# Sixty-four bytes: which columns of the low weight parts are displaced in the two feed-forward products of a hybrid decoder layer

## The chip, the cores and the metric

The kernel runs on one core of one Trainium2 chip. The metric is device time in microseconds (us) of one execution; lower is better. TensorE multiplies, VectorE (DVE) and ScalarE (ACT) prepare operands and take results away, SyncE (SP) and GpSimd (POOL) issue transfers.

## What is computed

One decoder layer on 512 tokens of width 2048: adaLN modulation, a combined projection, a short convolution beside an attention with three branches, an output projection, and then the feed-forward part, in which the change lies:

```python
h = modulate(rms_norm(x, norm2_g[l]), sh2, sc2)
x = x + g2[:, None, :] * (jnp.square(jax.nn.relu(h @ w_ff1[l])) @ w_ff2[l])
return rms_norm(x, normf_g)
```

`w_ff1` is 2048 by 8192 and `w_ff2` 8192 by 2048, all in fp32.

## The kernel before

**Split numbers.** An fp32 operand is split into a high part (rounded to the type fp32r) and a low part (the rest). A product of two operands takes three matmuls, high by high, high by low and low by high (`mm3`, line 347). ScalarE writes the high part (`nc.scalar.activation(..., AF.Copy)`), VectorE the low part as the difference of the raw weight and the high part (`hilo`, line 1097).

**Seven products instead of eight.** Each feed-forward product is cut into blocks of two by two and done with seven block products (Winograd's form of Strassen's scheme): `operands` (line 1230) makes from four raw weight blocks seven operands, in the order B1, U6, T5, B2, T7, B3, T4, with four additions on VectorE (tiles `sg`, `rw`) and seven splits (tiles `hl`). Four raw blocks with their seven operands are called a pair here. The code counts pairs as `p` in the first product (`ff1`, line 1277; pairs 3 to 31, pairs 0 to 2 being done in another form by `part`, line 1347, with weights from `make`, line 1326) and as `4 * f + q` in the second (line 1443; pairs 0 to 30, the last block by `plain`, line 1421).

An operand is 128 rows by 8 blocks of 128 columns, k = 0 to 7. For each column block `run` (line 1246) issues three matmuls of 256 tokens, so an operand is 24 matmuls, a pair 168. The token tiles are `tk`, the accumulators `pf` (eight PSUM banks). In the second product the eight column blocks go to two results, four each.

**Where the weights lie.** The weight operands live in a ring of three tiles `hl` of 2048 + 64 fp32 numbers per partition (line 1046). The high part lies at the front, the low part 4096 bytes behind it. `SHIFT` is 16 numbers, 64 bytes. Three layouts exist, picked by `stage_of`: in the output projection (0) nothing is shifted; in the first feed-forward product (1) high and low are both shifted by 64 bytes, and in the third tile of the ring, the last column block of the low part lies 64 bytes further (`[1] * 7 + [2]`); in the second product (2) the third tile has its last four column blocks of the low part 64 bytes further (`[1] * 4 + [2] * 4`). So in the first product every third operand has one displaced column block, in the second every third has four. Class `Low` (line 1048) turns a column into its place. Where one column block is displaced, VectorE writes the low part in two instructions, of 896 and of 128 columns; where four are, one instruction with a two-part pattern does it (2 x 512). The split weights of the second half of the output projection (`kept`, line 1139) also use layout 1 for three tiles.

**What sets the order.** All instructions of this part are recorded by the class `Order` (line 47) and then emitted in the order that its planner finds: TensorE's order is the program's, the other engines take what is ready and most urgent, by cost formulas (`price`, line 91) and due times. Each engine then works strictly in its emitted order. An `hl` tile can be refilled only after TensorE has read it, three operands back; raw weights have six buffers (`rw`). In the second product VectorE also adds each result to the residual, six updates and one sum for each of two results in a pair (`update`, line 1384); in the last four blocks (`f == 7`) it adds the pieces of the final norm as well (`final`, `shared`). During the first pairs of the second product, SyncE also reads back the residual (`residual_pairs`, line 1409), and the last pieces of the first product (`outcome`, line 1260) are still being written.

Of the kernel before, what the change touches and what calls it, by code (L numbers as in the profile page):

```python
# [31 lines left out]
SHIFT = 16  # L32
# [241 lines left out]
def hybrid_layer(ctx: ExitStack, tc: tile.TileContext, a, out):  # L274
    nc = tc.nc
# [17 lines left out]
    nc = order = Order(tc, xs[0].tensor.tag, NMAIN, passes=6)  # L293
# [21 lines left out]
    class lane:  # L315

        def __init__(self, n):
            self.n = n
# [59 lines left out]
    ring = [slot(name="wa")[:, :1024] for _ in range(NWA)]  # L378
# [201 lines left out]
    w = weights(a["w_kv"][0])  # L580
# [8 lines left out]
    for s, (name, k) in enumerate(steps[:-1]):  # L589
# [6 lines left out]
        for n in range(8):  # L596
            c = slice(n * P, (n + 1) * P)
# [3 lines left out]
        if s + 1 < len(steps):  # L601

            nxt = steps[s + 1][1]
            if s >= 4:
                w = blob(s + 1)
# [3 lines left out]
            if s < 4:  # L609
                w = blob(s + 1)  # L610
# [152 lines left out]
    for j in range(8):  # L763
        if j % 2 == 0:
            ys.append(pair(name="y"))
        y = ys[-1][:, j % 2]
        got = []
        for i in range(3):
            n = 3 * j + i
# [30 lines left out]
    for g in range(NG):  # L800
        pv = [bank() for _ in range(NQ)]
        for blk in range(4):
            wh, wl = weights(a["w_v"][g * 4 + blk], BLOB)
            more_ada(1)
            for j in range(4):
                k = blk * 4 + j
                s = slice(j * 268, (j + 1) * 268)
                for t in range(NQ):
                    c = slice(t * P, (t + 1) * P)
# [5 lines left out]
        for t in range(NQ):  # L815
            if t % 2 == 0:
# [4 lines left out]
                                    in1=vv[g, t][:, 0].bitcast(F32), op=OP.subtract)  # L821
# [66 lines left out]
    nc = tc.nc  # L888
    temps = cycle(ts)
    nc = order = Order(tc, mix[0].tensor.tag, NMAIN, passes=6)  # L890
# [149 lines left out]
    nc = order = Order(tc, x1[0].tensor.tag, NMAIN)  # L1040
    ffn = ExitStack()
    ffp = ffn.enter_context(tc.tile_pool(name="ffp", bufs=2, reuse_waits="tile"))
    psf = ffn.enter_context(tc.tile_pool(name="psf", bufs=8, space=PSUM, reuse_waits="tile"))
    HT = T // 2
    rw = cycle([ffp.tile([P, 1024], F32, name="rw", bufs=6) for _ in range(6)])
    hl = [ffp.tile([P, 2048 + 4 * SHIFT], F32R, name="hl", bufs=3) for _ in range(3)]

    class Low:

        def __init__(self, t, places):  # L1050
            self.t, self.places = t, places

        def __getitem__(self, at):
            a, b = at[1].start, at[1].stop
            o = 1024 + self.places[a // P] * SHIFT
            return self.t[:, o + a:o + b]

        def parts(self):
            cut = [k for k in range(1, 8) if self.places[k] != self.places[k - 1]]
            if cut == [4]:  # L1060
                n = 512 + (self.places[4] - self.places[0]) * SHIFT
                o = 1024 + self.places[0] * SHIFT
                yield slice(0, 1024), self.t[:, o:o + 2 * n].rearrange("p (a b) -> p a b", a=2)[:, :, :512], 2
                return
            for a, b in zip([0] + cut, cut + [8]):
                c = slice(a * P, b * P)
                yield c, self[:, c], 1

    def ring(high, *low):
        return cycle([[t[:, high * SHIFT:high * SHIFT + 1024], Low(t, p)] for t, p in zip(hl, low)])  # L1070

    rings = [ring(0, [0] * 8, [0] * 8, [0] * 8), ring(1, [1] * 8, [1] * 8, [1] * 7 + [2]),
             ring(1, [1] * 8, [1] * 8, [1] * 4 + [2] * 4)]
    stage_of = [0]
    ffp.tile([P, SHIFT], F32, name="shift", bufs=1)
    sg = {t: cycle([ffp.tile([P, 1024], d, name="sg", bufs=2) for _ in range(2)])
          for t, d in (("first", F32R), ("sums", F32), ("last", F32R))}
# [13 lines left out]
        nc.sync.dma_start(out=raw, in_=src)  # L1091
        return raw

    def hl_tile():
        return [next(q) for q in rings][stage_of[0]]

    def hilo(dst, src, minus=False):
        nc.scalar.activation(dst[0], src, AF.Copy, scale=-1.0 if minus else 1.0)
        for c, low, n in dst[1].parts() if isinstance(dst[1], Low) else [(slice(0, 1024), dst[1], 1)]:
            x, h = src[:, c], dst[0][:, c].bitcast(F32)  # L1100
            if n > 1:
                x, h = (y.rearrange("p (a b) -> p a b", a=n) for y in (x, h))
            if minus:
                nc.vector.scalar_tensor_tensor(out=low, in0=x, scalar=-1.0, in1=h, op0=OP.mult, op1=OP.subtract)
            else:
                nc.vector.tensor_tensor(out=low, in0=x, in1=h, op=OP.subtract)
        return dst

    def square_into(sacc, xm, c, first):
# [25 lines left out]
        if i % 2:  # L1135
            nc.gpsimd.dma_start(out=x1d[i // 2], in_=x1[i // 2])

    stage_of[0] = 1
    kept = []
    for i in range(8):  # L1140
        if i < 3:
            dst = hl_tile()
        elif i == 3:
            dst = [next(sg["first"]) for _ in range(2)]
        elif i == 4:
            dst = [next(gt).rearrange("p a b c -> p (a b c)")
                   for _ in range(2)]
# [79 lines left out]
                tok[i][q] = tslot()  # L1227
                tsplit(tok[i][q], t)

    def operands(raw, minus=False):  # L1230

        a11, a21, a22, a12 = raw
        s1, s2 = [next(sg["sums"]) for _ in range(2)]
        sub(s1, a21, a22, OP.add)
        sub(s2, s1, a11, OP.add)
        yield hilo(hl_tile(), a11)
        yield hilo(hl_tile(), s2)
        yield hilo(hl_tile(), s1, minus)
        yield hilo(hl_tile(), a12)
        sub(a21, a21, a11, OP.add)  # L1240
        yield hilo(hl_tile(), a21)
        sub(s2, s2, a12, OP.add)
        yield hilo(hl_tile(), s2)
        yield hilo(hl_tile(), a22)

    def run(ps, w, toks, first, last, base=0, n=8, c=LO):
        wh, wl = w
# [29 lines left out]
    def ff1(p):  # L1277
        raw = [raw_blob(a["w_f1"][p, b]) for b in range(4)]
        ps = {}
        x, y = temp((P, 2, HT), name="gx"), temp((P, 2, HT), name="gy")  # L1280
        for i, w in enumerate(operands(raw, True)):
# [24 lines left out]
        outcome(p, x, y, [temp((P, 2, HT), name="gz") for _ in range(2)])  # L1306
# [19 lines left out]
    def make(n):  # L1326
        p, b = plan[n][:2]
        if n == 1:
            dst = [next(sg["first"]) for _ in range(2)]
        elif n == 3:  # L1330
            dst = [next(gt).rearrange("p a b c -> p (a b c)")
                   for _ in range(2)]
        else:
            dst = hl_tile()
        made[n] = hilo(dst, raw_blob(a["w_f1"][p, b]))

    def results_of(p):
# [101 lines left out]
                    final(m, halves[hf])  # L1439
            finish(hf)  # L1440

    stage_of[0] = 2
    for f in range(8):
        for i in range(7):
            for j in range(2):
# [5 lines left out]
        for q in range(3 if last else 4):  # L1451
            raw = [raw_blob(a["w_f2"][4 * f + q, b]) for b in range(4)]
            ps = [{}, {}]
            for i, w in enumerate(operands(raw)):
# [125 lines left out]
```

## Time and profile before

| what | value |
|---|---|
| time before, median of 3 runs | 2130.83 us (2130.73 to 2131.65) |
| the profiled execution's own time | 2131.37 us |
| its span, first to last instruction | 2129.6 us |
| mean granted TensorE clock | 0.991 |
| busy: TensorE, VectorE, ScalarE | 97%, 89%, 47% of the span |
| matmuls of 128 x 256 tokens on `hl` weights, `pf<-tk,hl` | 10704 |

How to read it: the profile of one execution gives for each instruction when it started and how long it took. The start is measured; the end of a matmul is modelled. Matmuls are pipelined, so one that lasts 276 ns does not keep the next waiting that long, and a busy TensorE says nothing about its pace: the pace is how many matmuls start in a stretch. A table by stretches of time gives each engine's busy time and, behind an x, the number of its instructions that touch the stretch. In it the first feed-forward product's full pairs run from about 930 to 1483 us, the second product from 1483 to about 2115 us.

### The profile page before, as it was taken

To read this page: it belongs to the slowest core of one execution; us is meant where nothing else is said; L and a number is where in the kernel's file an instruction comes from. 1 tells how busy PE (TensorE), PEld (TensorE's weight loads), DVE (VectorE), ACT (ScalarE), POOL (GpSimd) and SP (SyncE) were. 2 spreads that over 40 slices of the span, in tenths; PEclk is the share of its full clock that TensorE was granted. 3 is DMA by queue.
4 is the path that set the end of the run, shared out by engine and by line. 5 is a ranking of instruction groups with operands and counts; after the bars stand their busy time and mean duration, and the time that the engine had idled before them with its cause. 6 is when DMAs were issued, how large, how long until landed. Compare 5 with 4: busy or idle time off the path is not lost.

```text
span 2129.6 us, 38017 instructions
## 1 busy us (share of the span) xinstructions
PE 2071.7 (97%) x15014; PEld 1930.5 (91%) x15014; DVE 1889.5 (89%) x3045; ACT 1008.6 (47%) x1470; POOL 128.6 (6%) x244
## 2 busy tenths in 40 slices
PE   5999999999999999999999999999999999999997
PEld 3888778898877779999999999999999999999997
DVE  8989888887987656999999999999999999999998
ACT  4532333222454434766666666666433333333345
POOL 0000000000000001021221211111000000000000
PEclk8999999999999999999999999999999999999999
DMA  8995679888321144477766677669876366366452
GB/s 333 346 352 221 217 279 326 308 292 314 108 80 40 50 139 158 129 228 208 221 201 202 199 218 215 202 206 306 309 268 230 128 247 236 130 239 237 136 182 90
DMA packets 144130, 454.17 MB, mean 213 GB/s; under 512 B 15824, under 2 KB 20176, under 8 KB 143952
## 3 DMA queue, kind: packets, MB, share of 16 engines
q1 hardware_dynamic: 108816, 386.72, 52.5%
q0 software_dynamic: 34048, 63.98, 9.5%
q8 instruction: 118, 1.93, 0.4%
q10 hardware_dynamic: 1088, 1.05, 0.1%
q14 instruction: 60, 0.49, 0.1%
HBM read 383.53 MB, written 68.16 MB: 212 GB/s over the span
## 4 chain that ended last, share of the span: by engine, by line
PE 55%; DVE 1%; ACT 1%; issue 0%; DMA 0%; DVEq 0%; ACTq 0%
PE pf L120 55%; DVE x L120 0%; DVE hl L120 0%; ACT t L120 0%; ACT x L120 0%; DMA rw<-in_w_f 0%; DVE rw L120 0%; DVE sg L120 0%; DVE sacc L120 0%; ACT hl L120 0%; DVE t L120 0%; ACT tk L120 0%; DVE gt L120 0%; DVEq L1576 0%; ACT sacc L120 0%
## 5 line engine op out<-in xcount | busy, mean ns | idle before, releaser
L120 PE MATMUL pf<-tk,hl 128*128 128x256 f32 x10704 | 1235.5, 278 | 2.3 <-ACT t L120 1.4
L120 PEld LDWEIGHTS pf<-tk,hl 128*128 128x128 f32 x10704 | 1233.6, 188 | 3.1 <-ACT t L120 1.6
L120 ACT ACTIVATE hl<-rw 128x1024 fp32r<-128x1024 f32 x269 | 285.4, 1062 | 337.5 <-PE pf L120 302.7
L120 DVE TENSOR_TENSOR hl<-rw,hl 128x1024 fp32r<-128x1024 f32 (+2 forms) x314 | 331.9, 1064 | 36.5 <-ACT hl L120 36.5
L120 ACT ACTIVATE hl<-sg 128x1024 fp32r<-128x1024 f32 x180 | 191.1, 1062 | 230.1 <-PE pf L120 203.5
L120 PE MATMUL ps<-h_m,wh 128*128 128x512 f32 x1080 | 252.6, 390 | 0.0
L120 DVE SCALAR_TENSOR_TENSOR t<-wa,cs 128x1024 bf16<-128x1024 f32 x192 | 234.2, 1220 | 20.0 <-DMA wa<-in_w_ada 18.0
L120 PEld LDWEIGHTS ps<-h_m,wh 128*128 128x128 f32 x1080 | 201.6, 188 | 41.5
L120 ACT ACTIVATE wh<-raw 128x1024 fp32r<-128x1024 f32 (+1 forms) x106 | 112.7, 1063 | 251.8 <-PE ps L120 204.1
L120 DVE TENSOR_TENSOR hl<-sg,hl 128x1024 fp32r<-128x1024 f32 (+2 forms) x170 | 185.6, 1101 | 31.8 <-ACT hl L120 31.1
L120 PE MATMUL ps<-h,wh 128*128 128x512 f32 x840 | 200.7, 395 | 5.7 <-ACT h L120 3.3
L120 PEld LDWEIGHTS ps<-h,wh 128*128 128x128 f32 x840 | 159.1, 191 | 41.6 <-ACT h L120 5.3
L120 DVE TENSOR_TENSOR wh<-raw,wh 128x1024 fp32r<-128x1024 f32 (+1 forms) x106 | 129.9, 1226 | 24.3 <-ACT wh L120 23.5
L120 DVE SCALAR_TENSOR_TENSOR x<-pf,mod,x 128x256 f32<-128x256 f32 (+1 forms) x280 | 133.6, 486 | 17.7 <-PE pf L120 16.7
L120 DVE TENSOR_TENSOR sg<-sg,rw 128x1024 f32<-128x1024 f32 x120 | 146.0, 1217 | 0.1
L120 POOL DMA_DIRECT2D g<-gt x192 | 101.5, 533 | 408.6 <-ACT hl L120 237.7
L120 PE MATMUL pw<-mix,wh 128*128 128x512 f32 x384 | 109.8, 406 | 0.0
L120 ACT ACTIVATE t<-t 128x512 f32<-128x512 f32 (+3 forms) x131 | 74.7, 571 | 16.3 <-DVE t L120 14.3
L120 PEld LDWEIGHTS pw<-mix,wh 128*128 128x128 f32 x384 | 69.7, 190 | 11.0 <-issue 0.5
L120 DVE TENSOR_TENSOR sg<-rw 128x1024 f32<-128x1024 f32 x60 | 73.0, 1217 | 7.2 <-DMA rw<-in_w_f 4.8
L120 DVE TENSOR_TENSOR rw<-rw 128x1024 f32<-128x1024 f32 x60 | 72.9, 1216 | 0.0
L120 DVE TENSOR_TENSOR gt<-t,gt 128x512 fp32r<-128x512 f32 x96 | 65.5, 683 | 2.0 <-PE pf L120 1.1
(204 smaller groups left out, 1782.4 us busy)
## 6 DMA issues: line engine op xcount, KB each, us to landing
rw<-in_w_f SPq DMA_DIRECT2D x263, 512.0 KB, 3.9
wa<-in_w_ada SPq DMA_DIRECT2D x192, 512.0 KB, 6.0
tk<-g SPq DMA_DIRECT2D x114, 512.0 KB, 5.9
g<-gt POOLq DMA_DIRECT2D x192, 256.0 KB, 4.6
raw<-in_w_conv SPq DMA_DIRECT2D x32, 512.0 KB, 5.0
x<-in_xt SPq DMA_DIRECT2D x16, 512.0 KB, 5.3
raw<-in_w_kv SPq DMA_DIRECT2D x16, 512.0 KB, 4.6
raw<-in_w_cv SPq DMA_DIRECT2D x16, 512.0 KB, 3.8
```

Of the source, the lines that this page charges most:

```text
L120: x.i, x.eng, x.call = len(self.nodes), eng, (lambda: real(*args, **kw))
```

## The change

The three layouts go. There is one ring of three tiles, with a place (0 before the first feed-forward product, 1 from there on) that shifts high and low parts alike, and a flag per operand, `moved`: with it the last column block of the low part, and only that, lies 64 bytes further. It is set

- for the operands that `make` prepares (blocks 0 to 2 of the first product),
- for all seven operands of pairs with a number below 6: pairs 3, 4 and 5 of the first product, 0 to 5 of the second,
- for one operand in each later pair, operand i where i is the pair's number modulo 7,
- for no other: not for `kept`, and not in `plain`.

VectorE writes a moved low part in two instructions (896 and 128 columns), any other in one; the form 2 x 512 is gone. The core of the diff:

```diff
-    hl = [ffp.tile([P, 2048 + 4 * SHIFT], F32R, name="hl", bufs=3) for _ in range(3)]
+    hl = cycle([ffp.tile([P, 2048 + 4 * SHIFT], F32R, name="hl", bufs=3) for _ in range(3)])
...
-        def __getitem__(self, at):
-            a, b = at[1].start, at[1].stop
-            o = 1024 + self.places[a // P] * SHIFT
+        def __init__(self, t, at, moved):
+            self.t, self.at, self.moved = t, at, moved
+
+        def __getitem__(self, cols):
+            a, b = cols[1].start, cols[1].stop
+            o = self.at + (SHIFT if self.moved and a >= 7 * P else 0)
             return self.t[:, o + a:o + b]
...
+            return [slice(0, 7 * P), slice(7 * P, 8 * P)] if self.moved else [slice(0, 8 * P)]
...
-    rings = [ring(0, [0] * 8, [0] * 8, [0] * 8), ring(1, [1] * 8, [1] * 8, [1] * 7 + [2]),
-             ring(1, [1] * 8, [1] * 8, [1] * 4 + [2] * 4)]
...
-    def hl_tile():
-        return [next(q) for q in rings][stage_of[0]]
+    def hl_tile(moved=False):
+        t, o = next(hl), place[0] * SHIFT
+        return t[:, o:o + 1024], Low(t, 1024 + o, moved)
...
-    def operands(raw, minus=False):
+    def operands(raw, n, minus=False):
+
+        def tile(i):
+            return hl_tile(n < 6 or n % 7 == i)
...
-            dst = hl_tile()
+            dst = hl_tile(True)
```

TensorE's order of instructions stays as it was. The planner prices the two-instruction low parts by their sizes and so orders VectorE, and in places ScalarE, SyncE and GpSimd, anew. In the following rows, `hl` is the weight tile, `sg` a sum of raw blocks, `rw` a raw block, `pf` a result, and `x_5885` and `x_5886` tiles of the residual.

VectorE where the second product begins, before: the low parts of the first pair's operands and the first residual updates.

```order
L120 TENSOR_TENSOR hl<-sg,hl 128x1024
L120 TENSOR_TENSOR t<-t 128x256 x3
L120 TENSOR_TENSOR hl<-rw,hl 128x1024
L120 SCALAR_TENSOR_TENSOR x_5885<-pf,ngate,x_5885 128x256
L120 SCALAR_TENSOR_TENSOR x_5886<-pf,ngate,x_5886 128x256
L120 TENSOR_TENSOR hl<-rw,hl 128x2x512
L120 SCALAR_TENSOR_TENSOR x_5885<-pf,ngate,x_5885 128x256
L120 SCALAR_TENSOR_TENSOR x_5886<-pf,ngate,x_5886 128x256
L120 TENSOR_TENSOR hl<-sg,hl 128x1024
```

The same place in the changed kernel:

```order
L120 TENSOR_TENSOR hl<-sg,hl 128x896
L120 TENSOR_TENSOR hl<-sg,hl 128x128
L120 TENSOR_TENSOR t<-t 128x256 x3
L120 TENSOR_TENSOR hl<-rw,hl 128x896
L120 SCALAR_TENSOR_TENSOR x_5885<-pf,ngate,x_5885 128x256
L120 TENSOR_TENSOR hl<-rw,hl 128x128
L120 SCALAR_TENSOR_TENSOR x_5886<-pf,ngate,x_5886 128x256
L120 TENSOR_TENSOR hl<-rw,hl 128x896
L120 SCALAR_TENSOR_TENSOR x_5885<-pf,ngate,x_5885 128x256
L120 TENSOR_TENSOR hl<-rw,hl 128x128
L120 SCALAR_TENSOR_TENSOR x_5886<-pf,ngate,x_5886 128x256
```

Every low part has become two instructions, and the second sometimes stands behind a residual update.

VectorE in a later pair of the second product, as one piece of the difference:

```order
 L120 TENSOR_TENSOR sg<-sg,rw 128x1024
 L120 SCALAR_TENSOR_TENSOR x_5886<-pf,mod,x_5886 128x256
-L120 TENSOR_TENSOR hl<-sg,hl 128x2x512
+L120 TENSOR_TENSOR hl<-sg,hl 128x1024
 L120 TENSOR_TENSOR snap<-pf,snap 128x256
 L120 TENSOR_TENSOR sg<-rw 128x1024
```

There the instruction count stays and only the pattern of the written low part differs; one operand in such a pair is written in two pieces.

More of the change, by code (lines that the diff above doesn't have):

```diff
@@ L1045, in hybrid_layer @@
     rw = cycle([ffp.tile([P, 1024], F32, name="rw", bufs=6) for _ in range(6)])
-    hl = [ffp.tile([P, 2048 + 4 * SHIFT], F32R, name="hl", bufs=3) for _ in range(3)]
+    hl = cycle([ffp.tile([P, 2048 + 4 * SHIFT], F32R, name="hl", bufs=3) for _ in range(3)])
     class Low:
-        def __init__(self, t, places):
-            self.t, self.places = t, places
-        def __getitem__(self, at):
-            a, b = at[1].start, at[1].stop
-            o = 1024 + self.places[a // P] * SHIFT
+        def __init__(self, t, at, moved):
[3 more added lines that the diff above has]
+            o = self.at + (SHIFT if self.moved and a >= 7 * P else 0)
             return self.t[:, o + a:o + b]
         def parts(self):
[L1059 to L1070, printed above, removed]
-    rings = [ring(0, [0] * 8, [0] * 8, [0] * 8), ring(1, [1] * 8, [1] * 8, [1] * 7 + [2]),
-             ring(1, [1] * 8, [1] * 8, [1] * 4 + [2] * 4)]
-    stage_of = [0]
+            return [slice(0, 7 * P), slice(7 * P, 8 * P)] if self.moved else [slice(0, 8 * P)]
+    place = [0]
     ffp.tile([P, SHIFT], F32, name="shift", bufs=1)
@@ L1092, in raw_blob @@
         return raw
-    def hl_tile():
-        return [next(q) for q in rings][stage_of[0]]
+    def hl_tile(moved=False):
+        t, o = next(hl), place[0] * SHIFT
+        return t[:, o:o + 1024], Low(t, 1024 + o, moved)
     def hilo(dst, src, minus=False):
[L1098 to L1102, printed above, removed]
+        high, low = dst
+        nc.scalar.activation(high, src, AF.Copy, scale=-1.0 if minus else 1.0)
+        for c in low.parts() if isinstance(low, Low) else [slice(0, 1024)]:
+            x, h = src[:, c], high[:, c].bitcast(F32)
             if minus:
-                nc.vector.scalar_tensor_tensor(out=low, in0=x, scalar=-1.0, in1=h, op0=OP.mult, op1=OP.subtract)
+                nc.vector.scalar_tensor_tensor(out=low[:, c], in0=x, scalar=-1.0, in1=h,
+                                               op0=OP.mult, op1=OP.subtract)
             else:
-                nc.vector.tensor_tensor(out=low, in0=x, in1=h, op=OP.subtract)
+                nc.vector.tensor_tensor(out=low[:, c], in0=x, in1=h, op=OP.subtract)
         return dst
@@ L1136, in hybrid_layer @@
             nc.gpsimd.dma_start(out=x1d[i // 2], in_=x1[i // 2])
-    stage_of[0] = 1
+    place[0] = 1
     kept = []
@@ L1235, in operands @@
         sub(s2, s1, a11, OP.add)
[L1236 to L1239, printed above, removed]
+        yield hilo(tile(0), a11)
+        yield hilo(tile(1), s2)
+        yield hilo(tile(2), s1, minus)
+        yield hilo(tile(3), a12)
         sub(a21, a21, a11, OP.add)
-        yield hilo(hl_tile(), a21)
+        yield hilo(tile(4), a21)
         sub(s2, s2, a12, OP.add)
-        yield hilo(hl_tile(), s2)
-        yield hilo(hl_tile(), a22)
+        yield hilo(tile(5), s2)
+        yield hilo(tile(6), a22)
     def run(ps, w, toks, first, last, base=0, n=8, c=LO):
@@ L1280, in ff1 @@
         x, y = temp((P, 2, HT), name="gx"), temp((P, 2, HT), name="gy")
-        for i, w in enumerate(operands(raw, True)):
+        for i, w in enumerate(operands(raw, p, True)):
             ch, first, last = CHAIN[i]
@@ L1440, in plain @@
             finish(hf)
-    stage_of[0] = 2
     for f in range(8):
@@ L1453, in hybrid_layer @@
             ps = [{}, {}]
-            for i, w in enumerate(operands(raw)):
+            for i, w in enumerate(operands(raw, 4 * f + q)):
                 if f == 0 and q < 3 and i == B2:
```

## The prediction, made before the changed kernel was timed

> **What bounds the kernel now.** First the page's engine line, then the table by stretches, cut at places of the feed-forward part: first product (930 to 1483 us), pairs 0-1, 2-5, 6-27 and 28-30 of the second product, and the rest.
>
> ```profile
> span 2129.6 us, 38017 instructions
> PE 2071.7 (97%) x15014; PEld 1930.5 (91%) x15014; DVE 1889.5 (89%) x3045; ACT 1008.6 (47%) x1470; POOL 128.6 (6%) x244
> ...
> core 0: us, PE busy (x) PEld busy (x) DVE busy (x) ACT busy (x) POOL busy (x), PEclk, DMA share, GB/s
> 930.00:1483.00 553.00, 553.00 (x4870) 553.00 (x4869) 523.98 (x767) 355.41 (x495) 107.47 (x204) 1.00 0.70 214
> 1483.00:1522.76 39.76, 39.76 (x340) 39.75 (x339) 35.29 (x49) 17.88 (x23) 2.10 (x4) 1.00 0.89 334
> 1522.76:1602.32 79.56, 78.65 (x674) 78.18 (x673) 74.65 (x104) 32.11 (x34) 3.17 (x6) 1.00 0.76 272
> 1602.32:2033.66 431.34, 431.34 (x3699) 431.34 (x3697) 403.37 (x555) 163.67 (x154) 0.00 (x0) 1.00 0.58 202
> 2033.66:2092.56 58.90, 58.90 (x507) 58.90 (x506) 58.90 (x94) 31.97 (x46) 0.00 (x0) 1.00 0.33 110
> 2092.56:2129.60 37.04, 24.82 (x206) 23.72 (x204) 26.64 (x61) 17.50 (x45) 0.00 (x0) 0.87 0.32 114
> ```
>
> TensorE has no gap over almost the whole feed-forward part at full granted clock (1.00), so its pace is the time. The pace is not one number. A stretch's count takes in the two or three matmuls under way at its start. The first product: 553.00 us / 4867.6 = 113.61 ns a matmul. Pairs 6 to 27 of the second: 431.34 / 3696 = 116.70 ns. Same shape, same clock, no waits: 3.1 ns more, 2.7%.
>
> Where that comes from shows in the view of the tile `hl` on TensorE over short stretches (duration of a matmul, min/median/max, then first and last start): the whole first product, an undisplaced stretch in it, the end of an operand with a displaced column, and two stretches of pair 10 of the second product.
>
> ```profile
> engine op xcount: duration ns min/median/max, first and last start us, forms
> L120 PE MATMUL pf<-tk,hl x4826: 276/276/286, 931.8 to 1480.0; 128*128 128x256 f32 x194
> ...
> L120 PE MATMUL pf<-tk,hl x46: 276/276/276, 941.0 to 946.1; 128*128 128x256 f32 x46
> ...
> L120 PE MATMUL pf<-tk,hl x11: 276/276/286, 940.0 to 941.1; 128*128 128x256 f32 x11
> ...
> L120 PE MATMUL pf<-tk,hl x46: 276/276/276, 1693.4 to 1698.5; 128*128 128x256 f32 x46
> ...
> L120 PE MATMUL pf<-tk,hl x72: 277/281/286, 1683.4 to 1691.7; 128*128 128x256 f32 x72
> ```
>
> TensorE has two regimes, one with matmuls of 276 ns and one of 281 ns. The paces, from the table by stretches for the two stretches of pair 10:
>
> ```profile
> 1693.46:1698.90 5.44, 5.44 (x50) 5.44 (x49) 1.97 (x5) 0.00 (x0) 1.00 0.43 119
> 1683.60:1691.76 8.16, 8.16 (x72) 8.16 (x71) 2.44 (x7) 0.00 (x0) 1.00 0.35 104
> ```
>
> In the first 48 matmuls start (two more are under way): 113.3 ns. The second holds 69.6 in 8.16 us, 117 ns. Then the same view on `hl` in pair 3, before and after three operands with displaced columns (passed at 1548, 1556 and 1565 us):
>
> ```profile
> L120 PE MATMUL pf<-tk,hl x32: 276/276/276, 1543.8 to 1547.3; 128*128 128x256 f32 x32
> ...
> L120 PE MATMUL pf<-tk,hl x52: 277/281/283, 1549.0 to 1555.0; 128*128 128x256 f32 x52
> ...
> L120 PE MATMUL pf<-tk,hl x53: 281/281/281, 1557.4 to 1563.6; 128*128 128x256 f32 x53
> ...
> L120 PE MATMUL pf<-tk,hl x31: 276/276/276, 1567.8 to 1571.2; 128*128 128x256 f32 x31
> ```
>
> In the second of these rows 51 gaps take 6.0 us, 117.6 ns, in the third 52 take 6.2, 119 with the ends' rounding; I use 117.8, 4.5 ns over 113.3 as 281 is 5 over 276. Both regimes occur in the same code with the same operand shapes, and a run of either lasts until an operand with displaced columns passes, or a wait. So the regime is a phase that TensorE locks into, and displaced columns move the phase. One displaced column in the 276 regime is a short disturbance: matmuls of up to 286 ns around 941.0, then 46 of 276 sharp. The first product has one such column in every third operand and stays at 276 for all of its 553 us. The second product has four in every third operand, and these throw it out of the regime at the first, keep it out at the second and bring it back at the third, as in the four rows. The mean of 116.70 is that mixture.
>
> **The change, part by part.** I sum against the profiled execution, 2131.37 us, which is 0.54 above the median of 2130.83.
>
> *A displaced column in the 276 regime.* First product: 4867.6 x 113.33 ns = 551.65 us of the 553.00; the other 1.35 us over 68 displaced operands (every third of 203) is 20 ns each (16 to 24, one matmul of counting error).
>
> *Pairs 6 to 27 of the second product.* All get one displaced column a pair, the last of an operand, which is the first product's disturbance at a lower rate. If TensorE enters at 276 it stays: 3696 x 113.33 ns = 418.87 us, plus 22 x 20 ns = 0.44 us: 419.3 instead of 431.34. **-12.0 us.** VectorE can follow: it is busy 403.37 us there, and one split low part a pair costs little. Two pieces, 896 and 128 columns, against one of 1024:
>
> ```profile
> 1474.06 1.28 DVE L120 TENSOR_TENSOR hl<-sg,hl 128x896 fp32r<-128x896 f32 x2
> ...
> 1476.73 1.21 DVE L120 TENSOR_TENSOR hl<-rw,hl 128x1024 fp32r<-128x1024 f32 x1
> ```
>
> 1.28 - 1.21 = 0.07 us. 403.37 + 22 x 0.07 = 404.9 of 419.3 us, 96.6%; the first product runs without any wait at 523.98 of 553.00, 94.8%. The cover is 14 us in 22 pairs; if it were gone, VectorE would set the pace (a rival below).
>
> By the Trainium skill, "VectorE: DVE Perf Modes", section "The TRN2 errata — SBUF-src ops pay a fixed extra latency per instruction", an fp32 addition takes (N + 151) cycles at 0.96 GHz, so one more instruction would cost 0.157 us. Back to back the trace shows 0.07 us, since the next instruction starts before the last has ended; with 0.157 the next term would be 18 x 0.087 = 1.6 us worse.
>
> *Pairs 0 to 5 of the second product.* Here all seven low parts are split, and VectorE is late. By stretches, with its waits in 1483 to 1570 us and TensorE's in 1483 to 1602 us:
>
> ```profile
> 1499.32:1527.40 28.08, 28.08 (x241) 28.07 (x240) 28.08 (x37) 12.83 (x17) 2.64 (x5) 1.00 0.84 299
> 1527.40:1529.50 2.10, 2.10 (x21) 2.10 (x20) 0.05 (x1) 1.06 (x1) 0.00 (x0) 1.00 1.10 398
> 1529.50:1566.60 37.10, 36.19 (x308) 35.72 (x307) 36.97 (x51) 14.90 (x17) 2.64 (x5) 1.00 0.88 318
> ...
> DVE sg L120 <- DMA rw<-in_w_f: 3.1, 2, 2.1
> DVE sg L120 <- issue: 2.1, 1, 2.1
> ...
> PE pf L120 <- DVE hl L120: 0.9, 1, 0.9
> ```
>
> From 1499 to 1567 us VectorE has no idle time but one wait of 2.1 us for raw weights, with the transfers at their fullest (398 GB/s), and TensorE waits for a low part. A faster TensorE only waits longer there: what it would gain in pairs 0 to 3 is lost, and 18 split operands (pairs 1 and 2 and four of pair 3) put VectorE back by 18 x 0.07 = 1.3 us, or 0.6 if the wait at 1527 takes up the ten before it. I take 1.0. From the end of pair 3 VectorE is ahead again. Pairs 4 and 5 were
>
> ```profile
> 1563.22:1602.32 39.10, 39.10 (x338) 39.10 (x337) 36.36 (x52) 14.89 (x14) 0.00 (x0) 1.00 0.60 216
> ```
>
> 39.10 us and go at 168 x 113.33 + 7 x 20 ns = 19.18 each: -0.7. Together **+0.3** (-1.0 if waits hide all splits and part of the gain stays, +1.3 if nothing is won back).
>
> *Pairs 28 to 30 and the end.* In 2033.66 to 2092.56 us VectorE is busy 58.90 of 58.90 us, with the final norm's pieces. TensorE's later waits:
>
> ```profile
> PE pf L120 <- DVE sacc L120: 1.5, 1, 1.5
> PE pf L120 <- DVE t L120: 1.1, 1, 1.1
> ```
>
> It already waits for VectorE's sum of squares (`sacc`). Three pairs at 276 would save 3 x 0.55 us of TensorE's time, which goes into that wait: nothing gained, three splits lost. **+0.2** (-1.9 to +0.5).
>
> *First product and the blocks before it.* Displaced operands from pair 3 on fall from 68 to 21 + 26 = 47: -0.4 us. In `part` they rise from 6 to 20: +0.3. VectorE writes 12 more split parts for `make` and one less for `kept`: 11 x 0.07 = 0.8 us, in a stretch where TensorE waits for the second half's tokens, and where it begins at 281:
>
> ```profile
> PE pf L120 <- ACT t L120: 1.4, 1, 1.4
> ...
> L120 PE MATMUL pf<-tk,hl x23: 281/281/281, 861.0 to 863.6; 128*128 128x256 f32 x23
> ```
>
> Half of the 0.8 may show; a displaced column in every operand would end the 281 two operands sooner, 48 x 4.5 ns = 0.2 us. Together **0.0** (-0.6 to +0.8).
>
> The transfers move the same bytes; two raw blocks change places with a token or a residual tile in SyncE's queue, which I cost at nothing in pairs 6 to 27, where TensorE waits for no transfer, and leave to the bounds in pairs 0 to 5.
>
> Sum: -12.0 + 0.3 + 0.2 + 0.0 = -11.5 us: 2119.9 for the profiled execution, **2119.3** for the median.
>
> **The rivals.**
>
> *One displaced column a pair does not bring TensorE back (slower).* Price: if TensorE is at 281 when pair 6 begins and one column a pair only moves it from one 281 phase to another, a pair takes 168 x 117.8 + 20 ns = 19.81 us instead of 431.34 / 22 = 19.61: +4.4 over pairs 6 to 27, some +1.5 in pairs 0 to 5, +0.2 behind: 2136.9. For it speaks `kept` in the output projection, with one displaced column between these two stretches:
>
> ```profile
> L120 PE MATMUL pf<-mixa,hl x21: 281/281/281, 843.0 to 845.4; 128*128 128x256 f32 x21
> ...
> L120 PE MATMUL pf<-mixa,sg x23: 281/281/281, 846.0 to 848.6; 128*128 128x256 f32 x23
> ```
>
> One column did not end the 281 there. Against it: four columns do, every third time, so the phases are few; six pairs with seven such operands each give dozens of pushes, and from 276 one push is harmless 68 times of 68. It decides at the last wait in pairs 2 and 3. Chance 0.06.
>
> *The address does not matter to TensorE (no change).* Then the 281 stretches come from something else in the second product, its pace stays, and the splits are all that is left: 0 to +1.3 us, some 2131.5. Against it: both regimes within pair 10. Chance 0.04. The Trainium skill says this much in "TensorE: Matmul & The Clock Gate", sections "Back-to-back issue gap" and "Step-by-step: what each phase is for": a start-to-start gap of N / 2.4 + 2.5 ns, 109.2 for 256 columns, and separate read ports for weights and moving data, so that loading the next weights takes nothing from a running matmul. The trace does not agree: 113.3 ns at best, and 117.8 with equal shapes.
>
> *VectorE's waits do not shrink (half the gain).* In pairs 6 to 27 VectorE idles 431.34 - 403.37 = 28 us. If half of what TensorE gains returns as waits for low parts, -12.0 becomes -6.0: 2125.3. Against it the first product, with the same ring and VectorE as full. Chance 0.12.
>
> *More is gained.* Pairs 0 to 5 at -1.0 instead of +0.3 and the end at -1.4 instead of +0.2: -2.9, 2116.4. Chance 0.10.
>
> **How the numbers follow.** The forecast has the remaining 0.68, with 2117.5 to 2121.5 by its terms' bounds. The range takes in the better case and the one with half the gain, 2116.0 to 2125.5, and leaves out 0.10, a little more with the edges. Measurements of this kernel tell 0.2%, 4.3 us, from no change. Faster by more: forecast, better case and half gain (-5.5), 0.90. Same 0.04, slower 0.06.
>
> **What would show it.** The matmuls on `hl` in pairs 6 to 27 have a median of 276 ns in every pair, with a maximum near 286 once a pair; the stretch of these 22 pairs takes 419 us; pairs 0 to 5 still take about 119 us, with longer waits of TensorE for low parts; VectorE is busy 96 to 97% in pairs 6 to 27, and TensorE's wait for `sacc` near the end grows by one to two us. Wrong it would be with medians of 281 beyond pair 6, with TensorE idle between operands there, or with the time unchanged at 276 because VectorE sets the pace.

## The result and the profile after

| | median, us | runs |
|---|---|---|
| before | 2130.78 | 2128.90 to 2131.65, 4 runs |
| changed | 2117.88 | 2117.19 to 2121.09, 4 runs |

The ratio is 0.9944 (95% interval 0.9926 to 0.9961): the changed kernel is faster by 0.6%, 12.9 us. The prediction was 2119.3 us. A ratio leaves out runs more than 1.5% above the fastest of their kernel, which touches experiment 1 alone. The profiled execution is the longest of the four, 2121.09 us, against 2131.37 for the profiled one before.

The page's head of the changed kernel:

```profile
span 2119.3 us, 38070 instructions
PE 2058.8 (97%) x15014; PEld 1913.5 (90%) x15014; DVE 1888.8 (89%) x3102; ACT 1009.4 (48%) x1470; POOL 128.2 (6%) x244
```

Its table by stretches, which begin and end with the same matmuls as those shown of before (there the second product's first matmul is at 1483.26 us, 0.26 behind the cut at 1483.00): first product from pair 3, then pairs 0-1, 2-5, 6-27 and 28-30 of the second, and the rest. Behind each stretch and its length stand busy us and (x) instructions of the engines, the granted clock, the DMA share and GB/s.

```profile
core 0: us, PE busy (x) PEld busy (x) DVE busy (x) ACT busy (x) POOL busy (x), PEclk, DMA share, GB/s
929.12:1482.40 553.28, 553.28 (x4874) 553.17 (x4873) 522.67 (x746) 355.38 (x495) 106.57 (x202) 1.00 0.70 215
1482.40:1520.84 38.44, 38.44 (x338) 38.42 (x337) 34.80 (x60) 17.86 (x23) 1.26 (x3) 1.00 0.91 341
1520.84:1601.40 80.56, 78.26 (x674) 77.22 (x673) 76.49 (x131) 32.11 (x34) 4.01 (x8) 1.00 0.77 263
1601.40:2022.12 420.72, 420.72 (x3699) 420.72 (x3698) 401.44 (x578) 163.92 (x154) 0.00 (x0) 1.00 0.59 208
2022.12:2079.31 57.19, 57.19 (x506) 57.19 (x505) 57.19 (x93) 30.72 (x43) 0.00 (x0) 1.00 0.34 113
2079.31:2119.30 39.99, 25.90 (x206) 24.47 (x204) 29.05 (x65) 19.16 (x49) 0.00 (x0) 0.87 0.30 106
```

The gain is in one row. Pairs 6 to 27 hold the same 3696 matmuls and take 420.72 instead of 431.34 us (-10.6), with the granted clock at 1.00 in both and VectorE no busier. Pairs 0 to 5 take 38.44 + 80.56 = 119.00 instead of 1602.32 - 1483.26 = 119.06 us. Everything from pair 28 on takes 97.18 instead of 95.94 (+1.2), and the second product begins 0.9 us earlier. Together -10.3, the difference of the two profiled executions.

Inside pairs 6 to 27 the view of `hl` on TensorE in four stretches (pairs 6 to 16; the end of 16 and half of 17; half of 17 to 18; the end of 18 to 27) shows where the last 1.4 us are:

```profile
L120 PE MATMUL pf<-tk,hl x1818: 275/276/287, 1601.8 to 1807.9; 128*128 128x256 f32 x182
...
L120 PE MATMUL pf<-tk,hl x113: 280/281/282, 1808.8 to 1821.9; 128*128 128x256 f32 x113
...
L120 PE MATMUL pf<-tk,hl x194: 276/281/283, 1822.8 to 1845.5; 128*128 128x256 f32 x194
...
L120 PE MATMUL pf<-tk,hl x1531: 275/276/287, 1848.3 to 2021.9; 128*128 128x256 f32 x192
```

The median is 276 ns except from 1808 to 1845 us. The times between starts of successive matmuls, in ns, worked out from the starts in the trace at that place, say why (| is the end of the operand):

```
pair 16, T4, start            1808.36: 161 115 117 117 119 118 117 118 118
pair 17, B2, displaced column 1822.30: 120 116 | 120 117 118 117 118 119 117
pair 18, T7, displaced column 1844.91: 120 116 | 117 114 113 113 114 113 114
```

At 1808.36 one matmul started 48 ns late, and from there on the pace was 118. The displaced column of pair 17 disturbed it for three or four matmuls and left it at 118; that of pair 18 brought back 113. The cause of the late matmul begins with a wait of VectorE, shown by the view of VectorE's waits from 1780 to 1820 us:

```profile
DVE sg L120 <- DMA rw<-in_w_f: 1.9, 1, 1.9
```

A raw weight block came 1.9 us late, and from there on VectorE ran without a gap. Its rows just before the late matmul (start and duration in us):

```profile
1806.62 1.21 DVE L120 TENSOR_TENSOR hl<-rw,hl 128x1024 fp32r<-128x1024 f32 x1
1807.75 0.86 DVE L120 SCALAR_TENSOR_TENSOR x<-pf,mod,x 128x256 f32<-128x256 f32 x2
```

The first row is the low part of T4, which was ready in time, at 1807.84 us. T4 adds to the results of T7, though, and a residual update has to read these first. The first of the two updates ended at 1808.23, and only then did T4's first weight load start, at 1808.29, some 40 ns late (worked out from the semaphore's times in the trace). So the regimes, how one is left and how it is entered again stand in one picture: 37 us at 281, some 313 matmuls x 4.5 ns = 1.4 us.

### The profile page after: what moved, and what is told of

Same layout as the page of the kernel before. It is cut to its first block, busy times and chain, and to the rows that moved or that the text cites. A ratio compares the mean times of both kernels' runs of the same rounds, so it can differ in the third digit from the quotient of the medians.

```text
span 2119.3 us, 38070 instructions
## 1 busy us (share of the span) xinstructions
PE 2058.8 (97%) x15014; PEld 1913.5 (90%) x15014; DVE 1888.8 (89%) x3102; ACT 1009.4 (48%) x1470; POOL 128.2 (6%) x244
## 4 chain that ended last, share of the span: by engine, by line
PE 73%; DVE 9%; DMA 3%; ACT 2%; issue 1%; DVEq 0%; SPq 0%; ACTq 0%
PE pf L120 56%; PE ps L120 11%; PE pw L120 3%; DVE hl L120 1%; PE pv L120 1%; DVE t L120 1%; DMA raw<-in_cmp_w 1%; DVE x L120 1%; PE s L120 1%; PE pt L120 1%; DVE nm L120 1%; DMA wa<-in_w_ada 1%; DVE wh L120 1%; DMA rw<-in_w_f 1%; DVE tk L120 1%
## 5 line engine op out<-in xcount | busy, mean ns | idle before, releaser
L120 PE MATMUL pf<-tk,hl 128*128 128x256 f32 x10704 | 1222.3, 277 | 2.8 <-DVE hl L120 2.5
L120 PEld LDWEIGHTS pf<-tk,hl 128*128 128x128 f32 x10704 | 1219.6, 188 | 4.4 <-DVE hl L120 3.7
L120 DVE SCALAR_TENSOR_TENSOR x<-pf,mod,x 128x256 f32<-128x256 f32 (+1 forms) x280 | 131.5, 482 | 14.6 <-PE pf L120 12.9
L120 DVE TENSOR_TENSOR sg<-rw 128x1024 f32<-128x1024 f32 x60 | 73.0, 1217 | 12.9 <-DMA rw<-in_w_f 10.2
L120 ACT ACTIVATE gt<-t 128x512 fp32r<-128x512 f32 x96 | 60.3, 629 | 16.7 <-DVE t L120 13.2
```

Source lines behind the costliest of these rows:

```text
L120: x.i, x.eng, x.call = len(self.nodes), eng, (lambda: real(*args, **kw))
```

## The experiments

**Theory.** TensorE's stream of 128 x 256 matmuls on `hl` weights has a fast phase (276 ns, pairs of 19.04 us) and slow phases (281 ns, pairs of 19.79 us). A wait of TensorE can put it from one into another. A displaced column in the fast phase costs some 20 ns and leaves it there; in a slow phase one displaced column, or a second one, leads back to the fast one. **Rivals:** what the diff does beside the address counts (the form 2 x 512 that goes, the split low parts, VectorE's order); or one displaced column a pair is not enough, and something else brought TensorE back. Each edit below is against the changed kernel.

**1. Nothing displaced** (`e1_none`).

```diff
-            return hl_tile(n < 6 or n % 7 == i)
+            return hl_tile()
...
-            dst = hl_tile(True)
+            dst = hl_tile()
```

> No low part is displaced anywhere, and every low part is written in one piece; the common shift of 64 bytes stays. Regime theory: nothing but a wait of TensorE moves it from one regime to the other, so long stretches without a wait are wholly at 276 ns or wholly at 281, with no disturbance once an operand. A pair takes 19.04 us at 276 and 19.79 at 281. If the waits before the first product and in pairs 1 to 4 of the second happen to leave 276, the whole takes 2116 to 2118 us; if they leave 281 in the second product, 25 x 0.73 = 18 us more, 2135; in both products, about 2155. Rival, the old layout is to blame (four displaced columns were the trouble and displacing is of no use): all pairs at 276 whatever the waits, 2116 us.

Ten runs: 2117.22, 2131.81, 2135.74, 2139.03, 2140.00, 2141.09, 2142.13, 2151.86, 2155.73 and 2158.41 us, median 2140.55; before 2129.07 on the same chip (13 runs). The ratio of 1.003 (1.0004 to 1.0056) is that of the seven shorter runs; the spread is the result, with the mean granted clock between 0.990 and 0.994 in all ten. The profiled run is the 2117.22. In it TensorE was at 276 through the whole first product, as `hl` on TensorE shows:

```profile
L120 PE MATMUL pf<-tk,hl x4873: 275/276/277, 925.8 to 1478.0; 128*128 128x256 f32 x195
```

So it was in the second product's pairs 6 to 27, in the table by stretches:

```profile
1598.39:2017.27 418.88, 418.88 (x3698) 418.88 (x3697) 399.53 (x554) 164.02 (x154) 0.00 (x0) 1.00 0.59 207
```

418.88 us for 22 pairs is the pace of 113.33 ns with nothing added, the number that the prediction used. So displacement does not make the fast phase; without it, the phase is left to chance, and one run in ten had the luck to the end. That the other nine ran at 281 in part is read from their times alone; experiment 2 has a trace of such a run. Sixty pairs at 281 would add 60 x 0.747 = 45 us, 2162 in all, which the longest run comes near.

**2. The same instructions, but the address** (`e4_split_only`). The low parts are written in the same two pieces, into a column that isn't displaced.

```diff
-            o = self.at + (SHIFT if self.moved and a >= 7 * P else 0)
+            o = self.at
```

> The same low parts as in the changed kernel are written in two pieces, by the same instructions in the same order, but nothing is displaced: only the address differs. Regime theory: as with nothing displaced, no disturbance once an operand, the regime is set by waits alone and stays: 2117 or, with a wait that leaves 281 in the second product, up to 2135, and in both products 2155. Rival, two instructions (their order, their semaphores) do it and not the address: the time and the 276 regime of the changed kernel, 2118, with the same recovery after waits.

Median 2153.88 us (2142.29, 2153.57, 2154.18, 2154.46), ratio 1.0101 (1.0074 to 1.0129), where the changed kernel has 0.9944: some 35 us (medians of different batches) by an address alone. In the profiled run, the stretches of the first product's pairs 6 to 31 and of the second's 6 to 27:

```profile
984.65:1499.10 514.45, 514.45 (x4370) 514.45 (x4369) 470.51 (x657) 318.35 (x445) 96.54 (x183) 1.00 0.67 208
1616.38:2043.65 427.27, 427.27 (x3698) 427.26 (x3697) 403.56 (x578) 163.77 (x154) 0.00 (x0) 1.00 0.58 205
```

The view of `hl` on TensorE in the second product, up to pair 16 and from pair 16 on:

```profile
L120 PE MATMUL pf<-tk,hl x1900: 275/276/277, 1589.7 to 1805.0; 128*128 128x256 f32 x190
...
L120 PE MATMUL pf<-tk,hl x2451: 275/281/357, 1811.8 to 2100.0; 128*128 128x256 f32 x189
```

514.45 us for 26 pairs is 19.787 a pair, 117.8 ns a matmul: the slow pace from end to end. Nothing ended it in 514 us. Later the waits of the second product's first pairs happened to lead to 276, until a wait in pair 16, the same place as in the changed kernel; from there it stayed at 281 to the last pair. The changed kernel was back after two displaced columns. The instructions of VectorE, ScalarE and GpSimd stand in the same order in both traces, so this rival is out.

**3. The selection in parts** (`e2_first_six`, `e3_one_each`).

```diff
-            return hl_tile(n < 6 or n % 7 == i)
+            return hl_tile(n < 6)
```

> Displaced columns only in the blocks before pair 3 and in the pairs below 6; none in the later pairs. Regime theory: pairs 6 and on run at 276 without any disturbance, 19.04 us each, 0.02 less than in the changed kernel, so 1 us less in all, 2116 to 2117; but a wait after pair 6, as the one in pair 16 of the changed kernel's profile, leaves TensorE at 281 to the end of the product, 0.73 us a pair. Rival, VectorE sets the gain: 0.07 us less a pair on VectorE changes nothing where it is not busy all the time, the same time as the changed kernel.

```diff
-            return hl_tile(n < 6 or n % 7 == i)
+            return hl_tile(n % 7 == i)
```

> One displaced operand a pair from the first pair on (the blocks before pair 3 keep all). Regime theory: after each wait in pairs 1 to 4 up to two pairs are at 281 until pushed back, so pairs 0 to 5 of the second product lose at most 3 x 0.73 us of TensorE's time, but they wait for VectorE anyway, and VectorE has six splits a pair less, 18 x 0.06 = 1.1 us where it is late; pairs 3 to 5 of the first product gain 15 x 0.02 = 0.3 us. Pairs 6 and on as in the changed kernel. Sum 0 to -1 us, 2116.5 to 2118. Rival, the first six pairs are needed in full: pairs 6 and on stay at 281, 2133 or more.

With the first six pairs alone: 2114.16, 2115.89, 2116.42, 2119.80 and 2132.13 us, median 2116.42, ratio 0.994 (0.9923 to 0.9957). With one operand a pair alone: 2114.90, 2116.34, 2120.73, 2121.15 us, median 2118.54 (0.5 above what I expected), ratio 0.9947 (0.993 to 0.9964). Both keep the gain at the median. The difference is the 2132.13, the profiled run of the first kernel. Its stretches of the first product's pairs 6 to 31 and the second's 6 to 27:

```profile
983.21:1497.66 514.45, 514.45 (x4370) 514.45 (x4369) 469.46 (x630) 318.76 (x445) 96.54 (x183) 1.00 0.67 208
1614.59:2033.48 418.89, 418.89 (x3698) 418.89 (x3697) 399.72 (x555) 164.01 (x154) 0.00 (x0) 1.00 0.60 208
```

It fell to 281 in pair 5 of the first product, with one displaced operand left, which was not enough, and stayed for 514 us; the displaced operands of the second product's first pairs ended it. So the one operand a pair is an insurance: it costs 0.02 us a pair, and saves up to 19 us in a run in which the luck fails. The full displacement of the first six pairs can't be told from nothing at the median: pairs 0 to 5 of the second product took 118.27 us without it.

**4. The old layout back in the second product** (`e5_old_second`).

```diff
-        t, o = next(hl), place[0] * SHIFT
+        (i, t), o = next(hl), place[0] * SHIFT
+        moved = 4 * (i == 2) if second[0] else 7 * moved
...
+            if isinstance(low, Low) and low.moved == 4:
+                n, o = 512 + SHIFT, low.at
+                to = low.t[:, o:o + 2 * n].rearrange("p (a b) -> p a b", a=2)[:, :, :512]
...
+    second[0] = 1
```

> The changed kernel with the second product's old layout put back: every third operand there has its last four column blocks displaced, written in one 2 x 512 piece; the first product stays as changed. Regime theory: the second product goes back to the cycle of nine operands, pairs 6 to 27 take 431 us (19.6 a pair), the whole gain is gone: some 2130. Rival, the gain came from the first product or from VectorE's new order: 2117 to 2122.

Median 2129.86 us (2127.30 to 2132.38, 10 runs) against 2128.32 (19 runs), ratio 1.0007 (0.9997 to 1.0016). The whole gain goes, and pairs 6 to 27 are where they were:

```profile
1599.83:2031.06 431.23, 431.23 (x3698) 431.23 (x3697) 402.94 (x555) 163.74 (x154) 0.00 (x0) 1.00 0.58 202
```

So the gain lies in the second product's layout, and what the change does to the first product is worth nothing that can be measured.

**5. All seven operands of every pair** (`e6_all_seven`).

```diff
-            return hl_tile(n < 6 or n % 7 == i)
+            return hl_tile(True)
```

> All seven operands of every pair have a displaced last column. Regime theory: never more than two operands at 281 after a wait, but each pair pays 7 x 20 ns: 19.18 us instead of 19.06, 51 later pairs x 0.12 = 6 us, 2122 to 2124, and a small spread from run to run. Rival, VectorE is the limit: six more splits of 0.06 us a pair, 98% busy in the second product, TensorE waits for low parts in most pairs and a pair takes over 19.3 us, 2130 or more.

Median 2125.96 us (2125.44 to 2131.40, 10 runs), ratio 0.9991 (0.9982 to 1.0001). It never stays at 281, but pays for each displaced column and loses most of the gain. Undisturbed pairs took 19.180 us in its trace, 19.060 in the changed kernel's, and 19.040 with none displaced: 0.020 us for each column. The second product's pairs 6 to 27:

```profile
1604.62:2026.58 421.96, 421.96 (x3698) 421.96 (x3697) 409.69 (x707) 163.81 (x154) 0.00 (x0) 1.00 0.59 207
```

421.96 - 418.88 = 3.1 us for 154 displaced columns, 20 ns each, just the price that the prediction had worked out from before; over both products 51 pairs have six columns more, 51 x 0.12 = 6.1 us. The medians, of different batches, lie 8.0 us apart, and the 2125.96 is above the 2122 to 2124 that I expected. In the first product TensorE also waited for VectorE, which it did not do in the changed kernel's trace:

```profile
PE pf L120 <- DVE t L120: 2.4, 3, 1.4
```

So the rival that VectorE becomes the limit had a small part there.

**6. Another distance** (`e7_by_32`, `e8_by_128`, `e10_by_128_again`, with the changed kernel itself beside it as `e9_after_again`).

```diff
-            o = self.at + (SHIFT if self.moved and a >= 7 * P else 0)
+            o = self.at + (SHIFT // 2 if self.moved and a >= 7 * P else 0)
```

> As the changed kernel, but the column is displaced by 32 bytes instead of 64. If the push goes with the distance, a displaced column at 276 costs less than 20 ns and one push moves the phase half as far, so that more operands are needed after a wait: pairs 0 to 5 may suffice, one a pair may take four pairs; 2116 to 2135. If any other address does, the same as the changed kernel: 19.06 us a pair, 20 ns a displaced operand, 2118.

```diff
-            o = self.at + (SHIFT if self.moved and a >= 7 * P else 0)
+            o = self.at + (2 * SHIFT if self.moved and a >= 7 * P else 0)
```

> As the changed kernel, but the column is displaced by 128 bytes. If what counts is the place within 128 bytes, nothing is displaced in that sense: 19.04 us a pair, no disturbance, no recovery after a wait, 2117 or 2135 or 2155 by luck, as with nothing displaced. If it is the distance, 20 ns or more an operand and a recovery at least as fast as with 64 bytes, 2118 to 2120.

> The changed kernel itself, unaltered, so that the distance of 128 bytes can be set against it on one chip. Both theories: a median of 2117 to 2120 us, single runs between 2115 and 2122, ratio to the kernel before 0.993 to 0.997.

> The same kernel with the displaced column 128 instead of 64 bytes further. In the profile of the first run at 128 bytes a displaced column cost nothing at 276 (pairs of 19.040 us, where 64 bytes makes 19.06), and every one of five stretches at 281 ended with the first displaced column, not with the second or third. Theory (only the phase counts): the undisturbed pairs again 19.040, no pair of the second product behind a wait at 281 for longer than to its displaced operand, and a median 0.5 to 2 us below the changed kernel's of this batch. Rival (the first run was lucky, the distance is of no account): medians within 0.5 us of each other. Rival (128 bytes does nothing to TensorE, like none displaced): runs spread from 2117 to 2158, median near 2140.

32 bytes: 2149.39 (profiled) and 2117.05 us, two runs, the first outside both ranges that I expected. Its first product's pairs 6 to 31, each with a displaced operand, stayed at 281 to the end, as with nothing displaced; the second fell in pair 16 and stayed:

```profile
990.70:1505.15 514.45, 514.45 (x4370) 514.45 (x4369) 470.25 (x657) 318.27 (x445) 96.57 (x183) 1.00 0.67 207
1623.41:2051.29 427.88, 427.88 (x3699) 427.68 (x3697) 403.38 (x578) 163.64 (x154) 0.00 (x0) 1.00 0.58 204
```

So it is not displacement as such that helps: a distance of 32 bytes costs TensorE 27 ns a column at 276 (undisturbed pairs of 19.067 us against 19.040), more than 64 bytes, and repairs next to nothing.

128 bytes: 2115.99 and 2120.10, then 2115.40 to 2119.99, median 2118.58 of 5; the changed kernel beside it 2117.98 (2116.02 to 2119.72, 6 runs), before 2128.14. Ratios 0.9951 (0.9938 to 0.9963) and 0.9948 (0.9936 to 0.996): no difference at the median, as the rival had it that the distance is of no account. In the trace it is of some: a column displaced by 128 bytes costs nothing at all (no matmul over 276 ns; first row, pairs 6 to 30), where 64 bytes shows its 286 (second row, the changed kernel):

```profile
L120 PE MATMUL pf<-tk,hl x4150: 276/276/276, 1604.8 to 2075.0; 128*128 128x256 f32 x198
```

```profile
L120 PE MATMUL pf<-tk,hl x3678: 276/276/286, 1599.8 to 2016.9; 128*128 128x256 f32 x194
```

That is 0.02 us a pair, 1 us in both products, too little to be told from the spread of the stages before. My 0.5 to 2 us did not show.

**7. Waits made on purpose** (`e11_wait_first_six`, `e12_wait`). VectorE repeats one addition four times at the start of pairs 12 and 20 of the second product; the first kernel also displaces in the first six pairs alone.

```diff
-        sub(s2, s1, a11, OP.add)
+        for _ in range(5 if n in (12, 20) and not minus else 1):
+            sub(s2, s1, a11, OP.add)
...
-            return hl_tile(n < 6 or n % 7 == i)
+            return hl_tile(n < 6)
```

> Displaced columns in the first six pairs only, and VectorE held up by four more additions (4 x 1.21 = 4.8 us) at the start of pairs 12 and 20 of both products, of the second only as far as this edit goes: low parts are ready 2 to 3 us ahead there, so TensorE should wait some 2 to 3 us in each of the two pairs. Theory (a wait moves the phase, only a displaced column brings it back): TensorE leaves 276 at a wait in pair 12 or 20 of the second product and stays at 281, 19.787 us a pair, for all pairs behind it, up to 30, unless the second wait happens to restore it. Rival (281 has nothing to do with waits and displacement, it passes by itself): the pairs after 12 and 20 are back at 19.040 within a pair or two.

> The changed kernel with the same four more additions at the start of pairs 12 and 20 of the second product. Theory: it waits there as the run with displaced columns in the first six pairs alone does, but no more than two pairs are at 281 after either wait, and from then on they take 19.045 to 19.075 us. Rival (one displaced column a pair does not bring TensorE back): 281 to the end of the second product.

2122.15 and 2125.76 us. TensorE waited in both pairs in both kernels, and the waits did not move it. TensorE's waits from 1700 to 2020 us in the first (us in total, times, longest):

```profile
PE pf L120 <- DVE hl L120: 2.4, 2, 1.2
```

The view of `hl` there, behind the first and behind the second wait:

```profile
L120 PE MATMUL pf<-tk,hl x1317: 276/276/276, 1721.8 to 1871.0; 128*128 128x256 f32 x189
...
L120 PE MATMUL pf<-tk,hl x1802: 276/276/276, 1875.8 to 2080.0; 128*128 128x256 f32 x181
```

That is a miss of my theory in the form in which I wrote it down: not every wait leads away from 276. These four didn't; the pairs took 20.50 to 20.57 us, the wait and nothing more. A wait draws a phase anew; what decides which one comes out is not shown. Length alone does not: in the traces counted below, waits of 0.30 to 0.40 us led twelve times to 276 and ten times to 281.

**The count over all traces.** To put the misses and hits together, I took from the traces of the changed kernel and of eleven of these runs (all but the old layout's) every wait that found TensorE at 276 in the two products, and every displaced column passed with no wait near it (mean of nine starts before and behind; worked out from the starts of the matmuls).

| | stays at or leaves to 276 | to 281 |
|---|---|---|
| a wait (over 36 ns) met at 276 | 51 | 32 |
| a 64-byte column met at 276 | 868 | 0 |
| a 64-byte column met at 281 | 15 | 8 |
| a 128-byte column met at 276 | 203 | 0 |
| a 128-byte column met at 281 | 8 | 1 |
| a 32-byte column met at 281 | 2 | 71 |

With 64 bytes the eight that stayed at 281 were never two in a row: the next one always led to 276. They also look different, as in the rows of pairs 17 and 18 above (starts 120 116 120 117 118, then 120 116 117 114 113). I read this as two slow phases, where a 64-byte column leads from the first to the second and from the second to the fast one; the reading rests on these 23 columns. Most of the waits stand within a dozen matmuls of a displaced column; of 22 that do not, 6 led to 281. The 32-byte columns met at 276 are not in the table: 36 stayed, and one led to 281.

## Why the prediction was right, point by point

- *Two regimes, moved by displaced columns and waits.* Right. The address alone makes 35 us (experiment 2). What I did not have is that a wait is a draw: 32 of 83 led to 281.
- *One column at 276 costs 20 ns and leaves TensorE there.* Right: 868 of 868, and 20 ns by experiments 1, 5 and 6.
- *Pairs 6 to 27, -12.0.* -10.6 in the profiled execution, since TensorE spent 37 us at 281 behind a raw block that came late. In the second profiled execution of the same kernel it did not fall, and the stretch took what was forecast, 419.3 us:

```profile
1598.84:2018.15 419.31, 419.31 (x3698) 419.31 (x3697) 400.97 (x578) 163.94 (x154) 0.00 (x0) 1.00 0.59 208
2018.15:2075.35 57.20, 57.20 (x507) 57.20 (x505) 57.20 (x93) 30.71 (x43) 0.00 (x0) 1.00 0.34 114
2075.35:2116.70 41.35, 26.80 (x206) 25.25 (x204) 29.16 (x65) 19.28 (x49) 0.00 (x0) 0.82 0.29 102
```

  I had cost raw blocks in SyncE's queue at nothing there "where TensorE waits for no transfer". That step was too simple: VectorE's waits for raw blocks in these pairs grew from 0.1 us before (last number of the first row) to 4.7 us after (second row), and the one in pair 16 showed, at 48 ns of wait and 1.4 us behind it.

```profile
L120 DVE TENSOR_TENSOR sg<-rw 128x1024 f32<-128x1024 f32 x22 | 26.7, 1214 | 0.1
...
L120 DVE TENSOR_TENSOR sg<-rw 128x1024 f32<-128x1024 f32 x22 | 26.7, 1215 | 4.7 <-DMA rw<-in_w_f 4.7
```

  That the median is 276 in every pair was wrong for pairs 17 and 18 of that run.
- *VectorE can follow.* Right: 401 of 420.7 us, and TensorE's view of waits has no row from 1601 to 2022 us. The rival of half the gain had no place.
- *Pairs 0 to 5, +0.3.* -0.06, and 119.52 - 119.06 = +0.5 in the second profiled execution. Right within what two executions differ by. TensorE's waits for low parts grew, as forecast, from 0.9 to

```profile
PE pf L120 <- DVE hl L120: 2.0, 2, 1.7
```

- *Pairs 28 to 30 and the end, +0.2.* Mis-sized: +1.2, outside its bounds (-1.9 to +0.5). The mechanism held: TensorE saves 58.90 - 57.19 = 1.7 us in three pairs and loses it to VectorE's sum of squares, whose wait grows from 1.5 us to

```profile
PE pf L120 <- DVE sacc L120: 3.1, 2, 1.6
```

  The step that failed was to take VectorE's end as fixed but for three splits. VectorE is busy from pair 28 on up to the last sums of squares, but for 0.5 to 0.7 us. The last of them for the first half of the tokens, before and after (start and duration in us, then the idle time ahead of it):

```profile
2105.27 0.43 DVE L120 TENSOR_TENSOR sacc<-sacc,t 128x256 f32<-128x256 f32 x1 [0.48 <-ACT t L120]
```

```profile
2094.43 0.43 DVE L120 TENSOR_TENSOR sacc<-sacc,t 128x256 f32<-128x256 f32 x1 [0.48 <-ACT t L120]
```

  From the start of pair 28 that is 2105.27 - 2033.66 = 71.6 us before and 2094.43 - 2022.12 = 72.3 after, 0.7 more: VectorE has more left to do when TensorE arrives there. Worked out from the starts of its instructions, 0.40 us of it is one more residual update in that stretch (30 of `x<-pf,mod,x` instead of 29), 0.13 two split low parts, and the rest short waits. The other 0.5 us lie behind it, in the last half's chain, with TensorE at 281 in `plain`, where nothing is displaced.
- *First product and before, 0.0.* -0.9; in the second profiled execution the stretch from the first matmul on `hl` to the second product took 622.64 us against 622.28 before. No effect to be told.
- *One displaced column does not bring TensorE back (rival).* True of the first one a third of the time, never of two: 23 columns met at 281, no stretch outlived the second. The row of `kept` that spoke for it looks like one of these first pushes: the starts at that column were 121 116 119 117 ns apart.
- *The address does not matter (rival).* Out, by experiment 2. The start-to-start gap that the prediction names beside it is, in the Trainium skill, "TensorE: Matmul & The Clock Gate", section "Back-to-back issue gap", that of an isolated matmul. So the 113.3 ns of this stream, with a weight load before each matmul, does not speak against it.

The median, 2117.88, lies 1.4 us below the forecast; the profiled execution, with its 1.4 us at 281, 1.2 us above the 2119.9 summed for it. The four terms came out at -0.9, -0.1, -10.6 and +1.2 in the profiled execution. Two readings of the prediction need a word. The lower bounds of its terms (-12.0 - 1.0 - 1.9 - 0.6) give 2115.3 for the median, not 2117.5, so that the better case lies inside them. And VectorE's wait at 1527 us, which it takes for one for raw weights, has the releaser "issue" in the view, which names no cause.

## What to carry to other kernels

Where a matmul stream without waits has two sharp durations for the same shape at the same granted clock, compare the pace (starts a stretch), not the busy time, and look for what switches between them; here the two differ by 4%. A rare, cheap disturbance that leads back to the fast phase is an insurance, and its worth shows in the spread of the runs, not in one profile: with nothing displaced, the one profiled run was the best of ten. Make it as rare as the waits allow, since at 64 bytes each costs 20 ns, and test its distance, since 32 bytes repaired next to nothing and 64 and 128 did.

## What was not expected of the hardware

A column displaced by 128 bytes costs nothing at 276 and led back from 281 at once in 8 of 9, while 32 bytes costs 27 ns, more than 64, and led back in 2 of 73. What in the chip has these phases, no run shows.

After the long wait for the sum of squares near the end, the granted clock fell in some executions, the second profiled one of the changed kernel among them. In the first 128-byte run 2.75 us lay between two starts on `hl`, with four short matmuls near the end of that time; then 2.77 us at a granted clock of 0.64, with starts 213 ns apart:

```profile
2090.63:2093.40 2.77, 2.77 (x15) 2.59 (x15) 1.53 (x4) 1.20 (x3) 0.00 (x0) 0.64 0.02 6
```

In the changed kernel's profiled execution the same stretch was 2.33 us, and the clock stayed. The Trainium skill, "TensorE: Matmul & The Clock Gate", section "What's actually happening", puts the fall to half rate behind an idle window of about 3.4 us, free-running; here 2.75 us was enough. The length alone does not tell, as two waits in pair 2 of the second product show. With nothing displaced, 2.32 us between two starts were followed by the first row; in the second profiled execution of the changed kernel, 2.97 us by the second:

```profile
1529.50:1532.50 3.00, 3.00 (x19) 3.00 (x19) 3.00 (x5) 0.00 (x0) 0.00 (x0) 0.62 0.72 254
```

```profile
1529.60:1535.00 5.40, 5.37 (x44) 5.17 (x44) 5.40 (x11) 1.58 (x2) 0.00 (x0) 1.00 0.75 258
```

So a stage that gains on TensorE and pays in one longer wait can lose about 1 us more: ten matmuls x 100 ns.
